# Block 2's depthwise convolution: three of its eight channel blocks as TensorE matmuls, and GpSimd's work moved out of the norm before it

## The chip, the core and the metric

The kernel runs on one core of one Trainium2 chip. The metric is the device time of one execution in microseconds (us). The engines are named as the profile names them: PE (TensorE), DVE (VectorE), ACT (ScalarE), POOL (GpSimd) and SP, whose queue issues the weight loads.

## What is computed

Two transformer blocks run over 256 tokens of 1024 features. The change lies at the end of block 1 and in the first half of block 2. There, as the reference has it:

```python
def conformer_conv(a, b, w_dw, b_dw, ln_g, ln_b, w_pw2, b_pw2):
    u = a * jax.nn.sigmoid(b)
    u = lax.conv_general_dilated(
        u, w_dw[:, None, :], window_strides=(1,), padding=[(CONV_TAPS - 1, 0)],
        dimension_numbers=('NWC', 'WIO', 'NWC'), feature_group_count=CONV_WIDTH) + b_dw
    u = jax.nn.silu(layer_norm(u, ln_g, ln_b))
    return u @ w_pw2 + b_pw2
```

The convolution is depthwise and causal, with 31 taps: each of the 1024 channels has its own 31 weights, and its output at a token is a sum over that token and the 30 before it. `a` and `b` are two slices of one projection of the normed activations; the same projection yields queries, keys, values and two gates. Differential attention runs beside the convolution, the two gated results are added, projected by `w_out` and added to the residual. A routed mixture of 64 experts closes the block.

## The kernel before, in words

**Stages.** Block 1 with its experts ends at about 415 us. Then come the gate that closes block 1 (`put_pg`, L1651), the norm that opens block 2, the projections, the convolution and the attention (about 416 to 702 us), the two output projections (to 756 us), and block 2's experts (to the end). All weights come over SP's queue in tiles of 1 MB through a ring; a tile's place is loaded again when the tile has been used.

**Pieces.** A projection is cut into pieces of half a weight tile. A piece first splits its weights in two (`parts`, L506): ACT rounds a 128x1024 half to fp32r (`whi`, L513) and another engine subtracts to get the low part (`wlo`, L514). Then 24 matmuls (L548 or L558) make hi times hi, hi times lo and lo times hi. The low part is DVE's by default; `split["eng"]` gives it to POOL in some places. `fill` runs the next piece and prepares the splits of the two behind it; `ready(n, eng)` prepares the first n queued pieces at once. There are three buffers of each part.

**Order.** Every engine runs its instructions in program order, and the order is written by hand. `step` (L1700) runs one piece and then some convolution taps; there is one `step` inside the norm, 15 in a first loop and 48 in a second (64 in all, numbered 0 to 63 below). The table `WHEN` at the top says how many taps follow each step (`v`, `v0` for DVE, `p`, `p0` for POOL) and at which step each part of the attention and of the layer norm is emitted. The pieces are, in order: 16 for the convolution's inputs (`cb`, `ca`), 40 for queries, keys, values and gates, 8 of the modulation vectors (`ada`). After the 64 steps come the two output projections.

**The convolution.** `put_ca` (L1715) writes `u`, two blocks of 128 channels at a time, and queues 31 taps for each block. Blocks 1, 2, 4, 5 and 7 are DVE's: the last tap is a `tensor_scalar` with the bias (L1691), the other 30 are a `scalar_tensor_tensor` each (L1693), 128x256 elements. Blocks 0, 3 and 6 (`ON_POOL`) take their first product from DVE; then, for each of 30 taps, ACT multiplies by the weight (`tap`, L1696) and POOL adds (L1697). `conv_end` flushes what is left, and POOL adds the blocks for the layer norm (`added`, L1925).

**The norm before it.** In the last `put_pg` (j = 3) DVE makes `h` (L1659), and just before that `ready(5, P)` lets POOL make the low part of the first `cb` piece. After the sums of squares, `ready(4, P)` lets POOL make the low part of the first `ca` piece; DVE and ACT write the scaled transposable copy `xp` (L414, L416) beside it. POOL then scales `h` in place (L1772).

**Queries and keys.** `put_qk` and `rotate` form a chain: ACT squares, DVE sums, POOL adds and takes a power (`rr`, L1788), DVE scales (`qn`, L1794), POOL rotates (L1799 to L1801), PE transposes (L1809).

Of the kernel before, what the change touches and what calls it, by code (L numbers as in the profile page):

```python
# [7 lines left out]
F32 = mybir.dt.float32  # L8
# [4 lines left out]
OP = mybir.AluOpType  # L13
# [3 lines left out]
T = 256  # L17
# [6 lines left out]
            v=(4, 4, 3, 3, 3, 4, 3, 3, 3, 4, 4, 4),  # L24
            p=(2, 2, 1, 2, 2, 3, 2, 1, 2, 3, 2, 1),
            v0=(3, 3, 3, 3, 3),
            p0=(2, 2, 2, 2, 2),
            pool=(12, 32),
# [9 lines left out]
AHEAD = 2  # L38
ON_POOL = (0, 3, 6)
TWO_PI = 6.283185307179586  # L40
# [155 lines left out]
def two_blocks(ctx, tc, I, out):  # L196
# [1284 lines left out]
    def pre_a():  # L1481

        dwT = pr.tile([128, 8, 34], F32, name="dwT")
        ps = wk([128, 8, 34], "dw")
        for j in range(8):
            PE.transpose(ps[:, j], pre["crow"][:, 128 * j:128 * j + 128], ident[0:34, 0:34])
        V.tensor_copy(dwT, ps)
        pT = pr.tile([128, 2, T], F32, name="pT", tag="pT")
        ps = wk([128, 2, T], "tr")
        for k in range(2):  # L1490
            for tt in range(2):
                PE.transpose(ps[:, k, 128 * tt:128 * tt + 128], pre["pin"][:, tt, 128 * k:128 * k + 128], ident)
        V.tensor_copy(pT, ps)
        V.tensor_scalar(pre["sub"], pre["sub"], 1.0 - 0.2, None, op0=OP.mult)
        lsum = pr.tile([128, 2], F32, name="lsum")
        lj = pr.tile([128, 64], F32, name="lj")
        lam4 = pre["lam4"]
        for i in range(2):
            V.scalar_tensor_tensor(lj, lam4[:, 2 * i], 1.0, lam4[:, 2 * i + 1], op0=OP.mult, op1=OP.mult,
                                   accum_out=lsum[:, i:i + 1])  # L1500
# [150 lines left out]
    def put_pg(j, ps):  # L1651
        c = slice(256 * j, 256 * j + 256)
        sg = t2.tile([128, 2, 256], F32, name="sg")
        S.activation(sg, ps, AF.Sigmoid)
        if j == 3:
            ready(5, P)
        V.tensor_tensor(sg, pps[0][:, :, c], sg, op=OP.mult)
# [21 lines left out]

    taps = {V: [], P: []}  # L1680

    def conv_some(eng, n):
        q = taps[eng]
        for _ in range(n):
            if not q:
                return
            i, tap = q[0].pop(0)
            q[:2] = [x for x in q[1::-1] if x]
            src, w = u[:, i, tap:tap + T], dwT[:, i, tap:tap + 1]
            if tap == 30:  # L1690
                V.tensor_scalar(acc[:, i], src, w, dwT[:, i, 31:32], op0=OP.mult, op1=OP.add)  # L1691
            elif eng is V:
                V.scalar_tensor_tensor(acc[:, i], src, w, acc[:, i], op0=OP.mult, op1=OP.add)  # L1693
            else:
                t = t2.tile([128, T], F32, name="tap", bufs=4)
                S.activation(t, src, AF.Copy, scale=w)  # L1696
                P.tensor_tensor(acc[:, i], acc[:, i], t, op=OP.add)  # L1697

    def step(n, v, p, eng=V):
        for _ in range(n):  # L1700
            split["eng"] = eng
            fill()
            split["eng"] = V
            conv_some(V, v)
            conv_some(P, p)

# [8 lines left out]
    def put_ca(j, ps):  # L1715
        V.tensor_tensor(u[:, 2 * j:2 * j + 2, 30:], ps, sgl.pop(j), op=OP.mult)
        for i in (2 * j, 2 * j + 1):
            eng = P if i in ON_POOL else V
            taps[eng].append([(i, tap) for tap in [30] + list(range(30))])

# [11 lines left out]
    put_proj()  # L1732
    fill(9)
    ssum = sm.tile([128, 2, 2], F32, name="ssum")
# [5 lines left out]
    P.tensor_tensor(r4, rt, halfneg[:, 0:2], op=OP.pow)  # L1740
    ready(4, P)
    r = sm.tile([128, 2], F32, name="rstd")
# [14 lines left out]
    for k, ps in turned(xp):  # L1757
        if k == 4:
            step(1, 0, 0)
# [6 lines left out]
    u = a2.tile([128, 8, 30 + T], F32, name="u")  # L1766
    P.memset(u[:, :, 0:30], 0.0)
    x_acc, acc = acc, a2.tile([128, 8, T], F32, name="acc")
    bpw = pr.tile([128, D], F32, name="bpw", tag="finalg")
    P.dma_start(out=bpw, in_=bcast_rows(l0("b_pw2_2")))  # L1770
    for tt in range(2):
        P.tensor_scalar(h[:, tt], h[:, tt], r[:, tt:tt + 1], None, op0=OP.mult)  # L1772

# [39 lines left out]
    vv = a2.tile([128, 2, D], F32, name="vv")  # L1813
    sgc = a2.tile([128, 2, D], F32, name="sgc")
    sga = a2.tile([128, 2, D], F32, name="sga")
    def put_gc(j, ps):
        S.activation(sgc[:, :, 256 * j:256 * j + 256], ps, AF.Tanh, scale=0.5)

# [12 lines left out]
    for n in range(15):  # L1831
        step(1, WHEN['v0'][n // 3], WHEN['p0'][n // 3])

# [170 lines left out]
    def conv_end():  # L2004
        conv_some(V, 1000)
        conv_some(P, 1000)
        ln_s()
# [13 lines left out]
    for n in range(48):  # L2021
        step(1, 0, 0, P if n in WHEN["pool"] else V)
        for fn, args in sorted(after.get(n, ()), key=lambda x: WHEN["rank"].index(x[0].__name__)):
            fn(*args)
        conv_some(V, WHEN["v"][n // 3] if n < 36 else 0)
        conv_some(P, WHEN["p"][n // 3] if n < 36 else 0)
    ln["m"] = [a2.tile([128, 8, T], F32R, name="xm" + n, tag=t) for n, t in (("hi", "kT"), ("lo", "xp"))]
# [182 lines left out]
```

## Time and profile before

| | us |
|---|---|
| median of 3 runs (1255.69 to 1259.72) | 1256.07 |
| the profiled execution | 1257.67 |
| its span, first to last instruction | 1255.9 |
| busy in the span: PE / DVE / ACT / POOL | 1128.7 / 598.4 / 412.2 / 243.8 |
| chain that ended last: PE / DMA / DVE / POOL | 50% / 27% / 15% / 3% |

The chain follows the work that ended last back from the final instruction, at each step to what released it. An engine's busy time is an average over stages, so the stage that the change touches is read by itself. Matmuls are pipelined: one lasts longer than the time until the next starts.

### The profile page before, as it was taken

To read this page: it belongs to the slowest core of one execution; us is meant where nothing else is said; L and a number is where in the kernel's file an instruction comes from. 1 tells how busy PE (TensorE), PEld (TensorE's weight loads), DVE (VectorE), ACT (ScalarE), POOL (GpSimd) and SP (SyncE) were. 2 spreads that over 40 slices of the span, in tenths; PEclk is the share of its full clock that TensorE was granted. 3 is DMA by queue.
4 is the path that set the end of the run, shared out by engine and by line. 5 is a ranking of instruction groups with operands and counts; after the bars stand their busy time and mean duration, and the time that the engine had idled before them with its cause. 6 is when DMAs were issued, how large, how long until landed. Compare 5 with 4: busy or idle time off the path is not lost.

```text
span 1255.9 us, 22423 instructions
## 1 busy us (share of the span) xinstructions
PE 1128.7 (90%) x8571; PEld 751.2 (60%) x8571; DVE 598.4 (48%) x1303; ACT 412.2 (33%) x823; POOL 243.8 (19%) x300
## 2 busy tenths in 40 slices
PE   6999989996777779888887898999999999998997
PEld 5998765652324678887877795444444444344443
DVE  5764652331110679999997765222322222221223
ACT  4464441210101666665655443112111111111111
POOL 5020140000000156694965511000000000000000
PEclk9999999998788989999989898999999999998999
DMA  9874889999999764434433959799999999999995
GB/s 284 250 246 155 327 299 345 390 419 418 419 419 398 262 210 168 156 115 133 134 102 107 357 202 399 312 400 421 420 421 421 420 420 421 420 420 420 420 420 218
DMA packets 115789, 398.34 MB, mean 317 GB/s; under 512 B 7681, under 2 KB 67181, under 8 KB 79440
## 3 DMA queue, kind: packets, MB, share of 16 engines
q1 hardware_dynamic: 113216, 392.72, 80.5%
q0 software_dynamic: 2448, 4.03, 1.4%
q8 instruction: 70, 1.15, 0.4%
q14 instruction: 55, 0.45, 0.1%
HBM read 395.63 MB, written 1.06 MB: 316 GB/s over the span
## 4 chain that ended last, share of the span: by engine, by line
PE 50%; DMA 27%; DVE 15%; POOL 3%; issue 3%; ACT 2%; SPq 0%; ACTq 0%; POOLq 0%; DVEq 0%
DMA w<-in_w_exp_gu_dram 12%; PE gu L1255 10%; PE fk L548 9%; PE dn L1306 7%; DVE acc L1693 4%; DMA w<-in_w_up_dram 4%; DVE wlo L514 4%; PE fk L558 4%; PE ga L1222 4%; DMA w<-in_w_exp_down_dram 3%; DMA w<-in_w_gate_dram 3%; PE y L1315 3%; DMA w<-in_w_down_dram 3%; PE gu L1264 3%; PE ak L548 1%
## 5 line engine op out<-in xcount | busy, mean ns | idle before, releaser
L1255 PE MATMUL gu<-w,xg 128*32 128x512 f32 (+2 forms) x1440 | 208.0, 600 | 9.7 <-DMA w<-in_w_exp_gu_dram 9.6
L1277 DVE SCALAR_TENSOR_TENSOR hh<-sg,wslot,gu 128x256 f32<-128x256 f32 x38 | 25.8, 678 | 281.7 <-ACT sg L1275 281.7
L514 DVE TENSOR_TENSOR wlo<-w,whi 128x1024 fp32r<-128x1024 f32 (+2 forms) x111 | 140.8, 1278 | 36.2 <-ACT whi L513 36.1
L1255 PEld LDWEIGHTS gu<-w,xg 128*32 128x32 f32 (+2 forms) x1440 | 63.7, 118 | 149.5 <-issue 136.2
L1306 PE MATMUL dn<-w,hT 128*32 128x512 f32 (+2 forms) x976 | 151.0, 605 | 2.0 <-DMA w<-in_w_down_dram 1.6
L513 ACT ACTIVATE whi<-w 128x1024 fp32r<-128x1024 f32 (+2 forms) x116 | 118.8, 1032 | 41.9 <-PE fk L548 23.0
L1264 PE MATMUL gu<-w,xg 128*32 128x256 f32 (+1 forms) x1024 | 93.0, 436 | 32.2 <-DMA w<-in_w_gate_dram 13.3
L1275 ACT ACTIVATE sg<-gu 128x256 f32<-128x256 f32 x38 | 14.6, 384 | 314.1 <-PE gu L1255 202.6
L1309 DVE TENSOR_TENSOR ylo<-dn,yhi 128x512 fp32r<-128x512 f32 x76 | 52.6, 692 | 127.0 <-ACT yhi L1308 127.0
L548 PE MATMUL fk<-wlo,x4hi 128*128 128x256 f32 x320 | 93.3, 291 | 13.0 <-DVE wlo L514 12.2
L548 PE MATMUL fk<-whi,x4hi 128*128 128x256 f32 x320 | 94.6, 296 | 3.7 <-DVE qn L1794 3.3
L1697 POOL TENSOR_TENSOR acc<-acc,tap 128x256 f32<-128x256 f32 x90 | 85.7, 967 | 48.2 <-ACT tap L1696 43.0
L1264 PEld LDWEIGHTS gu<-w,xg 128*32 128x32 f32 (+1 forms) x1024 | 48.3, 132 | 76.7 <-issue 22.3
L548 PE MATMUL fk<-whi,x4lo 128*128 128x256 f32 x320 | 91.9, 287 | 0.0
L1693 DVE SCALAR_TENSOR_TENSOR acc<-u,dwT,acc 128x256 f32<-128x256 f32 x150 | 89.8, 641 | 0.8
L2168 POOL DMA_DIRECT2D w<-gd x1 | 0.6, 638 | 460.4 <-DMA w<-in_w_exp_gu_dram 460.4
L1306 PEld LDWEIGHTS dn<-w,hT 128*32 128x32 f32 (+2 forms) x976 | 40.5, 118 | 78.2 <-issue 70.8
L1308 ACT ACTIVATE yhi<-dn 128x512 fp32r<-128x512 f32 x76 | 45.4, 597 | 121.9 <-PE dn L1306 121.9
L548 PEld LDWEIGHTS fk<-wlo,x4hi 128*128 128x128 f32 x320 | 62.8, 196 | 15.0 <-DVE wlo L514 13.9
L1315 PE MATMUL y<-yhi,dT 128*128 128x512 f32 x152 | 64.7, 426 | 1.7 <-ACT yhi L1308 1.5
L548 PEld LDWEIGHTS fk<-whi,x4hi 128*128 128x128 f32 x320 | 62.9, 197 | 4.6 <-ACT vv L1827 2.0
L548 PEld LDWEIGHTS fk<-whi,x4lo 128*128 128x128 f32 x320 | 62.9, 197 | 0.0
(604 smaller groups left out, 2316.5 us busy)
## 6 DMA issues: line engine op xcount, KB each, us to landing
w<-in_w_exp_gu_dram SPq DMA_DIRECT2D x128, 1024.0 KB, 19.8
w<-in_w_exp_down_dram SPq DMA_DIRECT2D x60, 1024.0 KB, 19.8
w<-in_w_in_dram SPq DMA_DIRECT2D x37, 1024.0 KB, 5.4
w<-in_w_gate_dram SPq DMA_DIRECT2D x32, 1024.0 KB, 18.4
w<-in_w_up_dram SPq DMA_DIRECT2D x32, 1024.0 KB, 17.5
w<-in_w_down_dram SPq DMA_DIRECT2D x28, 1024.0 KB, 19.5
w<-in_w_ada_dram SPq DMA_DIRECT2D x24, 1024.0 KB, 5.1
w<-in_w_down_dram SPq DMA_DIRECT2D x8, 512.0 KB, 13.6
```

The costliest lines, as they stand in the source:

```text
L513: S.activation(hi, w, AF.Copy)
L514: split.get("eng", V).tensor_tensor(lo, w, hi.bitcast(F32), op=OP.subtract)
L548: PE.matmul(ps[:, tt, :n], lhsT=xs[a], rhs=w[b][:, k], skip_group_check=True, start=(i + tt + k + m == 0), stop=(i == 1 and k == 3 and m = ...
L558: PE.matmul(ps[:m, b], lhsT=w[a][:, k, m * b:m * b + m], rhs=x[c][:, 4 * i + k], skip_group_check=True, start=(i + b + k + z == 0), stop=( ...
L1222: PE.matmul(ps[:, j], lhsT=xx[:, tt, k], rhs=d[:, tt], start=(i == 0), stop=(i == 3))
L1255: PE.matmul(ps[off:off + w, :], lhsT=xg[:, k, o + off:o + off + w], rhs=gu_of(q0 + qi, k), start=(k == 0), stop=(k == 7))
L1264: PE.matmul(ps[off:off + w, 256 * part:256 * part + 256], lhsT=xg[:, k, o + off:o + off + w], rhs=of(q0 + qi, k), start=(k == 0), stop=(k ...
L1306: PE.matmul(ps[off:off + w, :], lhsT=hT[g][:, k, off:off + w], rhs=down_of(q0 + qi, k, f, last), start=(k == 0), stop=(k == 1))
L1309: V.tensor_tensor(lo[:, f], ps, hi[:, f].bitcast(F32), op=OP.subtract)
L1315: PE.matmul(y[tt][f], lhsT=DT[g][:, 128 * tt:128 * tt + 128], rhs=v[:, f], start=False, stop=(g == NG - 1 and i == 1), skip_group_check=True)
L1693: V.scalar_tensor_tensor(acc[:, i], src, w, acc[:, i], op0=OP.mult, op1=OP.add)
L1697: P.tensor_tensor(acc[:, i], acc[:, i], t, op=OP.add)
```

## The change

Blocks 0, 3 and 6 of the convolution become matmuls. For each of them POOL's queue copies `u` to DRAM and reads it back four times, shifted by 0 to 3 tokens, so that 128 partitions hold 4 shifts of 32 channels; POOL multiplies the tap weights into diagonal 32x32 matrices; 32 matmuls (8 groups of 4 taps, 4 groups of 32 channels) sum all taps into PSUM, and ACT adds the bias on the way out. They are emitted at steps 9, 15 and 22. The layout of the weights (`w4`) is made once during block 1's experts. ACT's and POOL's 90 taps and DVE's first products of these blocks go.

In the norm, the low part of the first `cb` piece is made by DVE and earlier (`ready(7, V)` after five fills), that of the first `ca` piece by DVE (`ready(4, V)`), and POOL's scaling of `h` is moved to after the eleventh step of the first loop. The gate tile `sgc` takes the memory of `u4` afterwards.

```diff
-            p=(2, 2, 1, 2, 2, 3, 2, 1, 2, 3, 2, 1),
-            p0=(2, 2, 2, 2, 2),
+            conv={9: 0, 15: 1, 22: 2},
...
+        for j in range(4):
+            for m in range(4):
+                PE.matmul(ps[32 * m:32 * m + 32, j], lhsT=ident[:, 32 * j:32 * j + 32],
+                          rhs=dwT[:, ON_PE[0]:ON_PE[-1] + 1:ON_PE[1] - ON_PE[0], m:m + 29:4], start=True, stop=True)
+        w4 = pr.tile([128, 4, n, 8], F32, name="w4")
+        V.tensor_copy(w4, ps)
...
-        if j == 3:
-            ready(5, P)
...
-                t = t2.tile([128, T], F32, name="tap", bufs=4)
-                S.activation(t, src, AF.Copy, scale=w)
-                P.tensor_tensor(acc[:, i], acc[:, i], t, op=OP.add)
...
+    def conv_load(n):
+        ud = gd.tile([128, UW], F32, name=f"ud{n}")
+        P.dma_start(out=ud, in_=u[:, ON_PE[n]])
+        u4 = a2.tile([128, 2, D], F32, name="u4", tag="sgc").rearrange("p a b -> p (a b)")[:, 0:4 * (T + 28)]
+        u4 = u4.rearrange("p (j t) -> p j t", j=4)
+        w = t2.tile([128, 8, 4, 32], F32, name="cw", bufs=1)
+        for m in range(4):
+            P.dma_start(out=u4[32 * m:32 * m + 32], in_=ud.rearrange("(j c) t -> c j t", j=4)[:, :, m:m + T + 28])
+        P.tensor_tensor(w, pre["w4"][:, :, n].rearrange("p j g -> p g j")[:, :, :, None].to_broadcast([128, 8, 4, 32]),
+                        pre["each"][:, None, None, :].to_broadcast([128, 8, 4, 32]), op=OP.mult)
+        cw[n] = u4, w
+
+    def conv_pe(n):
+        u4, w = cw.pop(n)
+        i = ON_PE[n]
+        ps = wk([128, T], "cv")
+        for g in range(8):
+            for j in range(4):
+                PE.matmul(ps[32 * j:32 * j + 32], lhsT=w[:, g, j], rhs=u4[:, j, 4 * g:4 * g + T], start=(g == 0), stop=(g == 7))
+        S.activation(acc[:, i], ps, AF.Identity, bias=dwT[:, i, 31:32])
+        if n + 1 in cw_due:
+            cw_due.remove(n + 1)
+            conv_load(n + 1)
...
-            conv_some(V, v)
-            conv_some(P, p)
+            if steps[0] in WHEN["conv"]:
+                conv_pe(WHEN["conv"][steps[0]])
+            steps[0] += 1
+            conv_some(v)
...
-    fill(9)
+    fill(5)
+    ready(7, V)
+    fill(4)
...
-    ready(4, P)
+    ready(4, V)
...
-    for tt in range(2):
-        P.tensor_scalar(h[:, tt], h[:, tt], r[:, tt:tt + 1], None, op0=OP.mult)
...
-        step(1, WHEN['v0'][n // 3], WHEN['p0'][n // 3])
+        step(1, WHEN['v0'][n // 3])
+        if n == 10:
+            for tt in range(2):
+                P.tensor_scalar(h[:, tt], h[:, tt], r[:, tt:tt + 1], None, op0=OP.mult)
```

`put_ca` calls `conv_load` for block 0 at step 3; block 3 is loaded when block 0's matmuls have been emitted (step 9), block 6 after block 3's (step 15).

## Rows read from the trace of the kernel before

**Rows 1.** Busy time by stretch: PE, weight loads, DVE, ACT, POOL; granted clock; DMA share

```profile
225.00:230.00 5.00, 5.00 (x39) 3.26 (x35) 0.79 (x2) 0.38 (x1) 0.00 (x0) 1.00 1.00 392
465.00:688.00 223.00, 193.33 (x1540) 182.35 (x1542) 209.51 (x346) 131.73 (x278) 149.48 (x178) 0.98 0.40 133
641.00:688.00 47.00, 40.43 (x313) 38.49 (x317) 39.47 (x71) 20.53 (x49) 26.38 (x26) 0.91 0.34 112
756.00:1256.00 500.00, 480.33 (x3200) 228.43 (x3200) 146.50 (x422) 91.06 (x179) 4.03 (x3) 0.98 0.97 398
```

**Rows 2.** Waits of PE, 465 to 520 us and 520 to 688 us

```profile
PE fk L558 <- DVE wlo L514: 2.5, 5, 1.2
PE fk L548 <- DVE wlo L514: 1.1, 1, 1.1
...
PE fk L548 <- DVE wlo L514: 11.0, 7, 4.0
PE qt L1809 <- POOL qn L1801: 5.7, 6, 1.8
PE fk L548 <- DVE qn L1794: 3.3, 3, 1.2
PE po L1898 <- ACT aT L1890: 2.0, 2, 1.2
PE pvar L1951 <- POOL lnsum L1930: 1.6, 1, 1.6
```

**Rows 3.** Groups of instructions by line and shape, 465 to 688 us

```profile
L1693 DVE SCALAR_TENSOR_TENSOR acc<-u,dwT,acc 128x256 f32<-128x256 f32 x150 | 89.8, 641 | 0.8
L1697 POOL TENSOR_TENSOR acc<-acc,tap 128x256 f32<-128x256 f32 x90 | 85.7, 967 | 48.2 <-ACT tap L1696 43.0 <-ACT whi L513 3.6
L514 DVE TENSOR_TENSOR wlo<-w,whi 128x1024 fp32r<-128x1024 f32 x51 | 69.1, 1357 | 4.6 <-ACT whi L513 4.6
L1696 ACT ACTIVATE tap<-u,dwT 128x256 f32<-128x256 f32 x90 | 41.7, 509 | 14.2 <-POOL acc L1697 9.0 <-DVE u L1716 5.2
L514 POOL TENSOR_TENSOR wlo<-w,whi 128x1024 fp32r<-128x1024 f32 x2 | 4.9, 2460 | 0.0
```

**Rows 4.** DVE in order of time: start, duration, engine, line, operation

```profile
504.20 1.26 DVE L1693 SCALAR_TENSOR_TENSOR acc<-u,dwT,acc 128x256 f32<-128x256 f32 x3
505.38 1.21 DVE L514 TENSOR_TENSOR wlo<-w,whi 128x1024 fp32r<-128x1024 f32 x1
...
512.20 2.73 DVE L1693 SCALAR_TENSOR_TENSOR acc<-u,dwT,acc 128x256 f32<-128x256 f32 x3
```

**Rows 5.** POOL in order of time, same columns, and the idle time before

```profile
509.23 6.30 POOL L1697 TENSOR_TENSOR acc<-acc,tap 128x256 f32<-128x256 f32 x6 [6.97 <-ACT tap L1696]
```

**Rows 6.** The chain that ended last, from 689 us: start, duration, what

```profile
689.84 1.91 PE ad L898 x32
```

**Rows 7.** DVE around the norms in order of time, as rows 4

```profile
449.57 0.69 DVE L1658 TENSOR_TENSOR sg<-sg,h 128x512 f32<-128x512 f32 x1
450.30 2.74 DVE L1659 TENSOR_TENSOR h<-sg,finalg 128x512 f32<-128x512 f32 x1
...
455.09 3.39 DVE L414 TENSOR_SCALAR xp<-h,r 128x512 f32<-128x512 f32 x2 [0.83 <-POOL r L1740]
...
755.77 1.28 DVE L414 TENSOR_SCALAR xp<-h,rstd 128x512 f32<-128x512 f32 x2 [1.13 <-POOL rstd L384]
```

**Rows 8.** POOL in the norm, in order of time, as rows 5

```profile
449.78 2.71 POOL L514 TENSOR_TENSOR wlo<-w,whi 128x1024 fp32r<-128x1024 f32 x1 [1.75 <-ACT whi L513]
...
460.13 0.57 POOL L1770 DMA_DIRECT2D bpw<-in_b_pw_dram  x1
460.73 5.70 POOL L1772 TENSOR_SCALAR h<-h,rstd 128x1024 f32<-128x1024 f32 x2
```

**Rows 9.** DMA issues of POOL's queue: size each, median us from issue to landing

```profile
finalg<-in_final_g_dram POOLq DMA_DIRECT2D x1, 512.0 KB, 9.1
bpw<-in_b_pw_dram POOLq DMA_DIRECT2D x1, 512.0 KB, 4.0
```

More of the change, by code (lines that the diff above doesn't have):

```diff
@@ L38 @@
 AHEAD = 2
-ON_POOL = (0, 3, 6)
+ON_PE = (0, 3, 6)
 TWO_PI = 6.283185307179586
@@ L1487, in pre_a @@
         V.tensor_copy(dwT, ps)
+        n = len(ON_PE)
+        ps = wk([128, 4, n, 8], "w4")
+        for j in range(4):
[4 more added lines that the diff above has]
+        V.tensor_copy(w4, ps)
+        V.memset(w4[96:128, :, :, 7:8], 0.0)
+        each = pr.tile([128, 32], F32, name="each")
+        V.tensor_tensor(each, twice[:, 0:32], twice[:, 32:64], op=OP.add)
+        pre.update(w4=w4, each=each)
         pT = pr.tile([128, 2, T], F32, name="pT", tag="pT")
@@ L1677, in two_blocks, with conv_some @@
     queue(*ada(3, fk))
-    taps = {V: [], P: []}
-    def conv_some(eng, n):
-        q = taps[eng]
+    taps = []
+    def conv_some(n):
         for _ in range(n):
-            if not q:
+            if not taps:
                 return
-            i, tap = q[0].pop(0)
-            q[:2] = [x for x in q[1::-1] if x]
+            i, tap = taps[0].pop(0)
+            taps[:2] = [x for x in taps[1::-1] if x]
             src, w = u[:, i, tap:tap + T], dwT[:, i, tap:tap + 1]
@@ L1691, in conv_some, with step @@
                 V.tensor_scalar(acc[:, i], src, w, dwT[:, i, 31:32], op0=OP.mult, op1=OP.add)
-            elif eng is V:
+            else:
                 V.scalar_tensor_tensor(acc[:, i], src, w, acc[:, i], op0=OP.mult, op1=OP.add)
-            else:
-                t = t2.tile([128, T], F32, name="tap", bufs=4)
-                S.activation(t, src, AF.Copy, scale=w)
-                P.tensor_tensor(acc[:, i], acc[:, i], t, op=OP.add)
-    def step(n, v, p, eng=V):
+    UW = T + 32
+    cw = {}
+    def conv_load(n):
[20 more added lines that the diff above has]
+            conv_load(n + 1)
+    cw_due, steps = [], [0]
+    def step(n, v, eng=V):
         for _ in range(n):
@@ L1715, in put_ca @@
     def put_ca(j, ps):
-        V.tensor_tensor(u[:, 2 * j:2 * j + 2, 30:], ps, sgl.pop(j), op=OP.mult)
+        V.tensor_tensor(u[:, 2 * j:2 * j + 2, 30:30 + T], ps, sgl.pop(j), op=OP.mult)
         for i in (2 * j, 2 * j + 1):
-            eng = P if i in ON_POOL else V
-            taps[eng].append([(i, tap) for tap in [30] + list(range(30))])
+            if i not in ON_PE:
+                taps.append([(i, tap) for tap in [30] + list(range(30))])
+            elif ON_PE.index(i) == 0 or ON_PE.index(i) - 1 not in cw:
+                conv_load(ON_PE.index(i))
+            else:
+                cw_due.append(ON_PE.index(i))
     queue(*crossed(*(dense_feat(x4, (nm, j), 128, 2, lambda ps, j=j, put=put: put(j, ps))
@@ L1758, in two_blocks @@
         if k == 4:
-            step(1, 0, 0)
+            step(1, 0)
         S.activation(xs[0][:, k], ps, AF.Identity, scale=a1c[:, k:k + 1], bias=mod[:, 0, k:k + 1])
@@ L1765, in two_blocks @@
         V.tensor_tensor(xs[1][:, k], acc[:, k], xs[0][:, k].bitcast(F32), op=OP.subtract)
-    u = a2.tile([128, 8, 30 + T], F32, name="u")
+    u = a2.tile([128, 8, UW], F32, name="u")
     P.memset(u[:, :, 0:30], 0.0)
+    P.memset(u[:, :, 30 + T:], 0.0)
     x_acc, acc = acc, a2.tile([128, 8, T], F32, name="acc")
@@ L1813, in two_blocks @@
     vv = a2.tile([128, 2, D], F32, name="vv")
-    sgc = a2.tile([128, 2, D], F32, name="sgc")
     sga = a2.tile([128, 2, D], F32, name="sga")
+    ln = {}
     def put_gc(j, ps):
+        if j == 0:
+            ln["sgc"] = a2.tile([128, 2, D], F32, name="sgc")
+        sgc = ln["sgc"]
         S.activation(sgc[:, :, 256 * j:256 * j + 256], ps, AF.Tanh, scale=0.5)
@@ L1922, in two_blocks @@
     V.memset(onesf, 1.0 / D)
-    ln = {}
     def added(x):
@@ L1983, in put_pw @@
     def put_pw(j, ps):
+        sgc = ln["sgc"]
         c = slice(256 * j, 256 * j + 256)
@@ L2004, in conv_end @@
     def conv_end():
-        conv_some(V, 1000)
-        conv_some(P, 1000)
+        conv_some(1000)
         ln_s()
@@ L2021, in two_blocks @@
     for n in range(48):
-        step(1, 0, 0, P if n in WHEN["pool"] else V)
+        step(1, 0, P if n in WHEN["pool"] else V)
         for fn, args in sorted(after.get(n, ()), key=lambda x: WHEN["rank"].index(x[0].__name__)):
             fn(*args)
-        conv_some(V, WHEN["v"][n // 3] if n < 36 else 0)
-        conv_some(P, WHEN["p"][n // 3] if n < 36 else 0)
+        conv_some(WHEN["v"][n // 3] if n < 36 else 0)
     ln["m"] = [a2.tile([128, 8, T], F32R, name="xm" + n, tag=t) for n, t in (("hi", "kT"), ("lo", "xp"))]
```

## The prediction

> **What bounds the kernel now.** I read the busy time by stretch first. From 465 to 688 us the steps run: DVE is busy 209.51 of 223 us, PE 193.33, POOL 149.48 and ACT 131.73, and the DMA engines are at 0.40 [rows 1]. DVE is the fullest engine, but PE is close behind, so DVE's relief can give back only what PE loses: the 223 - 193.33 = 29.7 us in which PE idles. The waits of PE say on whom: low parts that DVE has late (2.5 + 1.1 + 11.0 = 14.6 us), the rotation of queries and keys (5.7 on POOL, 3.3 on DVE), attention on ACT (2.0) and a layer-norm sum on POOL (1.6) [rows 2]. Two of the waits for DVE are of 4 us, and behind them the granted clock falls: 0.91 as a mean from 641 to 688 us. At the half level, 1.2 GHz, half of the time is lost, so 47 x (1 - 0.91) = 4.2 us of PE's busy time there is slowness and no work [rows 1].
>
> After 756 us the DMA engines are at 0.97 for 500 us [rows 1]. That stretch is a stream of weights whose start is set by the stage before it, so a gain before 688 us should move the end by as much.
>
> **Why DVE is full.** The groups of instructions give 150 taps at a mean of 641 ns and 51 low parts at 1357 ns [rows 3]. In order of time the same forms have two durations. At 504.20 us three taps take 1.26 us and the low part after them 1.21; at 512.20 us three taps take 2.73 us [rows 4]. POOL is idle for 6.97 us up to 509.23 and then adds six taps in 6.30 us [rows 5]. So a DVE tap costs about 0.40 us beside an idle POOL (1.18 from the first start to the low part's start, over 3) and up to 0.88 beside a POOL tap.
>
> **The change, part by part.**
>
> *POOL's and ACT's taps go.* POOL sheds 90 additions, 85.7 us, ACT 90 products, 41.7 us [rows 3]. Neither is the fullest engine, so by themselves they are worth nothing; what counts is DVE. Were every DVE tap and low part undisturbed, the taps would take 150 x (0.56 - 0.40) = 24 us less (0.56 is the mean of 0.641 without the 0.08 by which the next instruction overlaps, as 504.20 + 1.26 overlaps 505.38 in rows 4) and the low parts 51 x (1.357 - 1.21) = 7.5 us, 32 us in all. But POOL keeps the rotation, the sums and some low parts. Its taps are 85.7 of its 149.48 us, 57%; some of the rest are powers of 8 elements that hardly touch memory, so I take two thirds, 21 us. DVE's 3 first products go too, 3 x 0.4.
>
> *What comes to POOL in the same stretch:* three weight products of 1024 elements, for which the nearest row is a low part on POOL, 2.46 us [rows 3], and the scaling of `h`, 5.70 us, moved from 460.73 us [rows 8] into step 11. That is 13 us which disturb DVE as the taps did, about 13 x 21/85.7 = 3 us of it back. DVE: 209.5 - 21 - 1 + 3 = 190 us.
>
> *PE gets three times 32 matmuls* with 32 weight columns and 256 moving columns, four column groups in turn. The `ad` matmuls are of this form: 32 took 1.91 us [rows 6]. So 3 x 1.91 = 5.7 us, all on the path, because PE runs in order and is next to full. ACT's evacuations, three of about half a microsecond by a tap's 509 ns [rows 3], hide in what ACT has shed.
>
> *PE then becomes the bound:* 193.33 - 4.2 + 5.7 = 194.8 us of work against DVE's 190. What idle time remains is the open number. The rotation, attention and sum waits (5.7 + 3.3 + 2.0 + 1.6 = 12.6) are chains over several engines; POOL's part of them loses its queue of taps, but PE arrives sooner and they are exposed for longer, so I leave them at 11. Of the 14.6 us on DVE's low parts I keep 3, and 1 for POOL's later answer behind the third load. Together 15 us. The ends are 0 (below that nothing can go, since idle time is not negative) and 29.7 with the clock's 4.2 (nothing relieved). I take 15, nearer to the sum of the chains than to either end. The stretch: 194.8 + 15 = 209.8 instead of 223, **13.2 us less**.
>
> *The norm before it.* DVE's last `h` took 2.74 us where the same size took 0.69 just before [rows 7], while POOL made a low part from 449.78 us [rows 8]. That low part is now made by DVE before the last gate arrives, so 2.05 us go. `xp` took 3.39 us for two beside POOL's next low part, 1.28 undisturbed at 755.77 [rows 7]: 2.1 us go. Ahead of it DVE gets that low part, 1.21 [rows 4]. Together 2.05 + 2.1 - 1.2 = **3 us**. ACT's share of the split is where it was.
>
> *The loads of the convolution* are a chain on POOL's queue: one copy to DRAM, a wait for its landing, four reads, one product. The trace has no such copy. The nearest row is a POOL load of 512 KB, 0.57 us to issue [rows 8] and 4.0 us to land [rows 9]; the slowest landing of its kind is 9.1 us [rows 9]. With those, 0.6 + 4.0 + 4 x 0.6 + 4.0 = 11 us, or 0.6 + 9.1 + 2.4 + 9.1 = 21 us. From the load's emission to its matmuls lie six steps (3 to 9, 9 to 15) or seven (15 to 22), each at least 24 matmuls: PE's 194.8 us over 56 steps are 3.5 us each, so 21 us. I take 11, since the DMA engines are as free as then, and cost the wait at nothing; the cover is those six pieces, and at the other end it is just used up. Behind the waits on POOL's queue stand the scaling of `h`, which nobody needs until the output projection, and at step 17 the first sum and power for the rotation: that is the 1 us above. Three loads of some 0.15 MB written and 0.6 MB read add about 2 MB to a stretch at 0.40; nothing.
>
> *The layout of the weights* adds 16 tiny matmuls and a wait for a DVE copy during block 1's experts, some 2 us of PE (16 at 1.91/32 [rows 6], and a wait taken as one low part's 1.2). At 225 to 230 us the DMA engines are at 1.00 [rows 1], so the weights behind it arrive no sooner: nothing, or 2 us if that queue ran dry.
>
> **Sum.** 1257.67 - 13.2 - 3 = 1241.5 for the profiled execution; its time is 1.6 above the median, so 1239.9, **1240 us**.
>
> **Rivals.**
>
> *The relief is only partly DVE's.* If POOL's remaining rotation disturbs as much for each microsecond as the taps, or the chains fill the idle time, 24 us stay idle: 194.8 + 24 = 218.8, 4.2 less, with the norm 7.2: 1249 us. For it: 9 of the waits are already POOL's and DVE's latency in the rotation. Against it: the largest two waits come where DVE is late with taps behind it.
>
> *Nothing is relieved.* DVE's long taps come from something other than POOL's additions; then PE's 5.7 us come on top and the norm's 3 go: 1259 us, no difference to be measured. Against it: rows 4 and 5 change together. That the change does not do what it says would look the same; the diff leaves no additions on POOL.
>
> *The loads are late,* and the time is worse than before. Each microsecond that a load exceeds 21 us stops PE, three times over, with every engine behind it. The gain of 16 us is used up when each is 5.4 us late, at a round trip of 26 us; from there it is slower. With landings of 13 us, 0.6 + 13 + 2.4 + 13 = 29 us, 8 us late each: 1240 + 24 = 1264 us. Against it: the landings of 4.0 us in this very stage [rows 9]. The Trainium skill (SBUF — State Buffer, "A bandwidth-pool intuition that's wrong") speaks for it: while DVE runs certain fp32 operations GpSimd is locked out of a port that it shares with DVE and cannot write the descriptors of a DMA on its queue, so that the transfer seems blocked. By that rule the load's issue, not its landing, would stretch, and the time would be the 1264 of this rival. The trace shows no sign of it so far: POOL issued its load at 460.13 us in 0.57 us [rows 8].
>
> **Chances.** Forecast 0.62, the partial relief 0.14, nothing 0.12, late loads 0.12. A measurement of this kernel can tell about 0.3%, 3.8 us, from no change: faster is under 1252.3, slower over 1259.8. Faster 0.62 + 0.14 = 0.76, same 0.12, slower 0.12. The range: below, PE's idle time falls to 6 us, 9 better than forecast: 1231. Above, it goes past the partial relief up to where nothing is relieved, short of it: 1257; left out are the late loads and the tails, under 0.2.
>
> **What would show each step.** DVE's taps in the stretch at a mean under 550 ns and its busy time near 190 us; PE's waits for low parts at about 3 us; the granted clock at 1.00 in it; `h` at 0.69 and `xp` at 1.3 us in the norm; 32 convolution matmuls in 1.9 us; the first of them waiting for no load. What would make the prediction wrong: taps that stay at 600 ns, a wait of PE for a load or for the weight product, rotation waits that grow by more than the low parts' shrink, or a stretch after 688 us that takes the gain back in waits for weights.

## The result, and the profile after

The kernel with the change takes 1238.05 us (median of 4, 1236.69 to 1239.81), the kernel before 1256.03 us beside it (median of 4): 18.0 us less. The ratio of the runs is 0.9846, 95% interval 0.9827 to 0.9865, which is 19.4 us; below, kernels are compared by such ratios. The profiled execution of after took 1236.69 us, the lowest of its four; that of before, 1257.67, lies 1.6 above its median. So the two profiles differ by 21.0 us, 3 more than the medians, and what is read from them below adds up to the larger number.

Busy time by stretch of the kernel after (columns as in [rows 1]): all steps, the first and second part of them, and the experts.

```profile
461.83:668.00 206.17, 198.47 (x1723) 186.67 (x1725) 179.54 (x343) 96.62 (x189) 83.39 (x106) 0.98 0.48 156
461.83:520.00 58.17, 58.17 (x553) 54.68 (x552) 47.46 (x71) 25.39 (x31) 20.48 (x21) 1.00 0.67 208
520.00:668.00 148.00, 140.31 (x1173) 132.00 (x1175) 132.08 (x273) 71.23 (x158) 62.90 (x86) 0.98 0.40 135
735.50:1235.00 499.50, 477.99 (x3200) 229.78 (x3200) 146.66 (x422) 92.10 (x180) 4.73 (x4) 0.98 0.97 399
```

PE's steps begin 3.3 us earlier than before, at 461.83. They took 222.2 us before (465.16 to 687.4, inside the stretch of [rows 1]) and take 206.17 now: 16 us less. That lead is kept: the experts' first `xp` starts at 736.23 us (in the chain below) instead of 755.77 [rows 7], 19.5 us earlier. The stream of the experts' weights keeps the DMA engines at 0.97 as before, and its end comes 20.9 us earlier (the span went from 1255.9 to 1235.0 us): a start that comes earlier moves the end by about as much. In the first 58 us PE has no idle time at all.

Waits of PE in the steps, of the kernel after (us in total, times, longest):

```profile
PE fk L547 <- DVE wlo L513: 3.6, 3, 2.4
PE pvar L2000 <- POOL lnsum L1979: 2.0, 1, 2.0
PE qt L1852 <- POOL qn L1844: 1.8, 2, 1.3
PE fk L547 <- ACT vv L1874: 0.4, 1, 0.4
```

These four are all (`wlo` is a low part, `lnsum` the layer norm's sum, `qn` a normed query or key, `vv` the values). Low parts that DVE has late cost 3.6 instead of 14.6 us, the rotation 1.8 instead of 9.0 [rows 2].

Groups of instructions of after in the steps (columns as in [rows 3]):

```profile
L1703 DVE SCALAR_TENSOR_TENSOR acc<-u,dwT,acc 128x256 f32<-128x256 f32 x150 | 75.0, 543 | 0.8
L513 DVE TENSOR_TENSOR wlo<-w,whi 128x1024 fp32r<-128x1024 f32 x51 | 62.5, 1228 | 13.7 <-ACT whi L512 13.7
...
L1727 PE MATMUL cv<-u,cw 128*32 128x256 f32 x192 | 11.0, 380 | 0.0
...
L1716 POOL DMA_DIRECT2D u<-ud x12 | 6.6, 558 | 15.9 <-PE cv L1727 6.8 <-PE fk L547 4.8 <-PE fk L557 4.3
...
L1717 POOL TENSOR_TENSOR cw<-w,each 128x1024 f32<-128x1024 f32 x3 | 6.1, 2031 | 0.0
```

The same 150 taps went from 641 to 543 ns, the same 51 low parts from 1357 to 1228. What DVE now waits for is ACT's rounding (13.7 us): it has caught up with its supplier. PE's matmuls of the convolution wait for nothing (0.0 in the last column).

DVE in the norm, in order of time, and POOL with the first load of the convolution (columns as in [rows 4] and [rows 5]):

```profile
450.63 0.69 DVE L1669 TENSOR_TENSOR h<-sg,finalg 128x512 f32<-128x512 f32 x1
...
452.98 1.23 DVE L513 TENSOR_TENSOR wlo<-w,whi 128x1024 fp32r<-128x1024 f32 x1 [0.24 <-ACT whi L512]
454.12 1.29 DVE L413 TENSOR_SCALAR xp<-h,r 128x512 f32<-128x512 f32 x2
```

```profile
471.75 0.55 POOL L1711 DMA_DIRECT2D ud<-u  x1 [13.95 <-issue]
476.63 2.22 POOL L1716 DMA_DIRECT2D u<-ud  x4 [4.33 <-PE fk L557]
478.88 2.02 POOL L1717 TENSOR_TENSOR cw<-w,each 128x1024 f32<-128x1024 f32 x1
```

`h` is down from 2.74 to 0.69 us and the two `xp` from 3.39 to 1.29 [rows 7]. In the first load, the reads start 4.9 us after the copy to DRAM was issued. The wait ahead of them is put down to a matmul that had long been done; it is the copy's landing (as the wait of 4.82 us in the cut kernel below shows, which is put down to it by name).

The chain that ended last, of after: the three blocks of the convolution, POOL's scalings at the end of the layer norm, and the start of the experts' stage.

```profile
487.74 3.59 PE cv L1727 x64
...
508.80 3.59 PE cv L1727 x64
...
534.74 3.59 PE cv L1727 x64
...
672.72 7.22 POOL acc L2021 x6
...
736.23 0.69 DVE xp L413
```

Each block of the convolution is 3.59 us of PE, in 64 records; the code issues 32 matmuls for it. So one such fp32 matmul leaves two records.

### The profile page after: what moved, and what is told of

It is laid out like the page before. It is cut to its first block, busy times and chain, and to the rows that moved or that the text cites. A ratio compares the mean times of both kernels' runs of the same rounds, so it can differ in the third digit from the quotient of the medians.

```text
span 1235.0 us, 22677 instructions
## 1 busy us (share of the span) xinstructions
PE 1131.1 (92%) x8795; PEld 757.5 (61%) x8795; DVE 565.9 (46%) x1305; ACT 377.7 (31%) x736; POOL 170.1 (14%) x227
## 4 chain that ended last, share of the span: by engine, by line
PE 33%; DMA 25%; DVE 9%; POOL 3%; ACT 2%; issue 2%; SPq 0%; ACTq 0%; POOLq 0%; DVEq 0%
DMA w<-in_w_exp_gu_dram 17%; PE gu L1254 8%; PE fk L547 6%; PE dn L1305 4%; PE fk L557 4%; DMA w<-in_w_up_dram 3%; PE y L1314 3%; DVE acc L1703 2%; PE ga L1221 2%; DVE wlo L513 2%; DMA w<-in_w_down_dram 2%; DMA w<-in_w_exp_down_dram 2%; DMA w<-in_w_gate_dram 2%; PE y L2119 1%; PE ak L547 1%
## 5 line engine op out<-in xcount | busy, mean ns | idle before, releaser
L513 DVE TENSOR_TENSOR wlo<-w,whi 128x1024 fp32r<-128x1024 f32 (+2 forms) x113 | 136.7, 1219 | 45.9 <-ACT whi L512 45.8
L1305 PE MATMUL dn<-w,hT 128*32 128x512 f32 (+2 forms) x976 | 148.0, 604 | 3.1 <-DMA w<-in_w_down_dram 2.8
L1274 ACT ACTIVATE sg<-gu 128x256 f32<-128x256 f32 x38 | 14.6, 385 | 313.1 <-PE gu L1254 202.8
L1703 DVE SCALAR_TENSOR_TENSOR acc<-u,dwT,acc 128x256 f32<-128x256 f32 x150 | 75.0, 543 | 0.8
L1221 PE MATMUL ga<-disp,xhi 128*128 128x256 f32 x304 | 63.3, 290 | 0.0
## 6 DMA issues: line engine op xcount, KB each, us to landing
w<-in_w_up_dram SPq DMA_DIRECT2D x32, 1024.0 KB, 17.3
```

The lines of the kernel that those rows point to most:

```text
L513: split.get("eng", V).tensor_tensor(lo, w, hi.bitcast(F32), op=OP.subtract)
L1221: PE.matmul(ps[:, j], lhsT=xx[:, tt, k], rhs=d[:, tt], start=(i == 0), stop=(i == 3))
L1305: PE.matmul(ps[off:off + w, :], lhsT=hT[g][:, k, off:off + w], rhs=down_of(q0 + qi, k, f, last), start=(k == 0), stop=(k == 1))
```

## The experiments

The theory: DVE was the fullest engine because POOL's additions hold it up; without them PE's waits go, and PE is next to full. Against it stood ACT's relief (90 products that the change takes away too), POOL's queue (the additions stood ahead of the rotation there), the norm, and late loads. Ratios are to the kernel before, run beside each on the same chip.

### The norm alone, and the convolution alone

The kernel before with the norm's edits (`norm_only`), and the kernel after with them undone (`conv_only`):

```diff
-        if j == 3:
-            ready(5, P)
...
-    fill(9)
+    fill(5)
+    ready(7, V)
+    fill(4)
...
-    ready(4, P)
+    ready(4, V)
...
-    for tt in range(2):
-        P.tensor_scalar(h[:, tt], h[:, tt], r[:, tt:tt + 1], None, op0=OP.mult)
...
+        if n == 10:
+            for tt in range(2):
+                P.tensor_scalar(h[:, tt], h[:, tt], r[:, tt:tt + 1], None, op0=OP.mult)
```

These are the edits of `norm_only`; `conv_only` is the kernel after with the same lines turned back.

> The kernel before with the norm's part of the change alone: the two low parts on DVE, and the scaling of h after step 11; the convolution as before. My theory: the norm gives 3 us (h at 0.69 instead of 2.74, two xp in 1.3 instead of 3.4, one low part of 1.2 inserted), and the moved scaling, 5.7 us of POOL, now disturbs DVE and delays POOL's taps in the steps, up to 3 us back: 1253 to 1256 us. Rival, that most of the 18 us comes from the norm: 1245 or less. Rival, that the norm's gain is lost again in the steps, where DVE is full: 1256.

> The changed kernel with the norm as before: the low parts on POOL, the scaling of h in the norm; the convolution as changed. My theory: the convolution gives the rest, about 15 of the 18 us: 1240 to 1243 us, with h at 2.7 and the two xp at 3.4 us again. Rival, that the two parts need each other (the steps are short of DVE and POOL either way): the two parts alone add up to clearly less than 18 us, and this one is at 1246 or more.

Measured: the norm alone 1255.91 us, 0.9985 (0.9972 to 0.9997); the convolution alone 1241.33 us, 0.9869 (0.9852 to 0.9886). That is 1.9 and 16.5 us, 18.4 together, against 19.4 for both (0.0154 of 1257). The parts add, within what the intervals leave open; both runs lie in the range of the theory, the norm alone at its upper end, where its second rival lies too. In `norm_only` `h` takes 0.69 and `xp` 1.3 us as they do in after, but the two scalings of `h`, which now stand among POOL's and DVE's taps, take 3494 ns each instead of 2.85 us [rows 8], and the taps 646 ns: some of what the norm gives up is paid back in the steps. Beside the change's emptier POOL they take 2.93 us each.

### Which of the removed parts relieves DVE

The kernel after, with 90 operations put back where the taps were: additions on POOL over tiles of their own (`pool_adds_back`), products on ACT into a scratch tile (`act_products_back`), and fills on POOL, which write as much and read nothing (`pool_memsets`). Nobody waits for any of them.

```diff
+    def more(n):
+        for _ in range(n):
+            if extra[0] and steps[0] > 4:
+                extra[0] -= 1
+                P.tensor_tensor(dum[0], dum[0], dum[1], op=OP.add)
...
             conv_some(v)
+            more(p)
```

`act_products_back` has this as its last line of `more`, and `pool_memsets` `P.memset(dum[0], 0.0)`:

```diff
+                S.activation(t2.tile([128, T], F32, name="tap", bufs=1), u[:, 1, 0:T], AF.Copy, scale=dwT[:, 1, 0:1])
```

> The changed kernel, with 90 additions of 128x256 given back to POOL, in the places of the old ones, on two tiles of POOL's own that nobody else touches. My theory: DVE's taps and low parts are slow because POOL's additions read and write memory at the same time, so the mean tap goes from 543 back to about 640 ns and DVE's busy time in the steps from 180 to about 205 us; PE then waits for low parts by 10 to 15 us again: 1249 to 1260 us. Rival, that the gain came from ACT being freed of its products: the taps stay under 560 ns and the time at 1238 to 1241. Rival, that it came from POOL's queue, whose additions stood ahead of the rotation: the taps stay, and only PE's waits for the rotation grow, 1241 to 1246.

> The changed kernel, with 90 products of 128x256 given back to ACT, in the places of the old ones, into a tile that nobody reads. My theory: ACT was at 132 of 223 us before and is at 97 of 206 now, and its products do not touch DVE's speed: the mean tap stays within 10 ns of 543 and the time at 1237 to 1242 us. Rival, that ACT's high parts came late behind the products and held up DVE and PE: 1246 us or more, with waits of DVE for high parts.

> The changed kernel with 90 memsets of 128x256 given to POOL in the places of the old additions; they write memory and read none. My theory, that POOL's reading and writing beside DVE is what slows DVE, says nothing on writes alone; two forms of it: if it is the reading, DVE's mean tap stays under 560 ns and the time at 1238 to 1243 us; if writing does as much, the tap goes over 600 ns and the time over 1247. Rival, that the time is lost because POOL's queue makes the loads and the rotation wait, whatever it runs: PE's waits for the rotation and for the query and key banks grow and the time is over 1247 with taps under 560 ns.

Measured: additions 1269.9 us, 1.0112 (1.0092 to 1.0133), 10 us above the expected range; products 1240.02 us, 0.9862 (0.9847 to 0.9876); fills 1240.79 us, 0.9862 (0.9845 to 0.9879), both in the range of the theory. The groups in the steps, first with the additions, then the products, then the fills:

```profile
L1703 DVE SCALAR_TENSOR_TENSOR acc<-u,dwT,acc 128x256 f32<-128x256 f32 x150 | 94.4, 671 | 0.8
L1741 POOL TENSOR_TENSOR dum<-dum,dum 128x256 f32<-128x256 f32 x90 | 82.8, 920 | 5.2
```

```profile
L1703 DVE SCALAR_TENSOR_TENSOR acc<-u,dwT,acc 128x256 f32<-128x256 f32 x150 | 72.9, 529 | 0.8
...
L1741 ACT ACTIVATE tap<-u,dwT 128x256 f32<-128x256 f32 x90 | 45.5, 506 | 1.5
```

```profile
L1703 DVE SCALAR_TENSOR_TENSOR acc<-u,dwT,acc 128x256 f32<-128x256 f32 x150 | 71.8, 521 | 0.8
...
L1741 POOL MEMSET dum<- 128x256 f32 x90 | 28.2, 313 | 3.8
```

The additions alone bring back the long taps, 671 ns, though they share no tile and no wait with DVE. ACT's products, as long as they were before (506 ns), leave the taps at 529. Low parts have a mean of 1327 ns in that kernel, but two of the 51 make the difference: one of 3.18 and one of 4.25 us that lie beside POOL's weight product and a scaling of `h`. The ACT rival falls. Ninety fills leave the taps at 521: it is POOL's reading of SBUF that costs DVE time. The order of time shows how, DVE then POOL with the additions, and DVE then POOL with the fills:

```profile
472.71 1.52 DVE L1703 SCALAR_TENSOR_TENSOR acc<-u,dwT,acc 128x256 f32<-128x256 f32 x3
...
477.88 4.93 DVE L1703 SCALAR_TENSOR_TENSOR acc<-u,dwT,acc 128x256 f32<-128x256 f32 x3
482.73 1.76 DVE L513 TENSOR_TENSOR wlo<-w,whi 128x1024 fp32r<-128x1024 f32 x1
```

```profile
477.91 1.99 POOL L1717 TENSOR_TENSOR cw<-w,each 128x1024 f32<-128x1024 f32 x1
479.84 1.64 POOL L1741 TENSOR_TENSOR dum<-dum,dum 128x256 f32<-128x256 f32 x2
...
481.79 8.53 POOL L1741 TENSOR_TENSOR dum<-dum,dum 128x256 f32<-128x256 f32 x8
```

```profile
483.81 1.22 DVE L513 TENSOR_TENSOR wlo<-w,whi 128x1024 fp32r<-128x1024 f32 x1
```

```profile
483.37 2.89 POOL L1741 MEMSET dum<- 128x256 f32 x8
```

Three taps take 1.52 us while POOL does nothing, and 4.93 us beside the weight product and the additions behind it. The product's 1.99 us, two additions of about 0.8 and three taps of 0.4 to 0.5 make 4.8 to 5.1 us: as if the two engines took turns, one whole instruction each. A low part takes 1.76 us beside additions and 1.22 beside fills. The Trainium skill (SBUF — State Buffer, "Who interferes with whom") says that a VectorE instruction with two inputs in SBUF contends with a GpSimd instruction that reads SBUF and not with one that only writes it. These rows agree. The Trainium skill (SBUF — State Buffer, "SBUF: two separate sides") also says that whichever starts first holds the shared port pair for its whole instruction. The product and the additions agree; POOL's scalings of `h` in after, which read SBUF too, do not:

```profile
495.92 5.85 POOL L1882 TENSOR_SCALAR h<-h,rstd 128x1024 f32<-128x1024 f32 x2
```

```profile
497.78 1.21 DVE L513 TENSOR_TENSOR wlo<-w,whi 128x1024 fp32r<-128x1024 f32 x1
```

A low part that lies almost whole inside the first scaling takes no longer than beside an idle POOL, and the scalings take 5.85 us instead of 5.67 (in `short_cover`, beside an idle DVE). So not every reading instruction of POOL holds DVE up; why these do not stays open.

The additions made the kernel slower than before, which had the same number of them. The longest waits of PE in that kernel:

```profile
PE fk L547 <- DVE wlo L513: 9.0, 3, 4.5
PE fk L547 <- DVE qn L1849: 6.7, 1, 6.7
```

Low parts are late again, and one `qn` costs 6.7 us: POOL has the loads and the weight products on top of the additions now, and q's power stands behind them. So the additions cost in two ways, through DVE's speed and through POOL's queue, and both come back with them. How the 19.4 us divide between the two is not shown: the fills keep POOL busy for 28.2 us where the additions keep it for 82.8, too little to load its queue as before. PE's waits fell by 11.0 us for low parts and by 7.2 for the rotation.

### Is PE the bound now?

Only the first of eight groups of taps is multiplied, 4 of 32 matmuls; loads and weight products stay (`conv_cut`).

```diff
-        for g in range(8):
+        for g in range(1):
...
-                PE.matmul(ps[32 * j:32 * j + 32], lhsT=w[:, g, j], rhs=u4[:, j, 4 * g:4 * g + T], start=(g == 0), stop=(g == 7))
+                PE.matmul(ps[32 * j:32 * j + 32], lhsT=w[:, g, j], rhs=u4[:, j, 4 * g:4 * g + T], start=True, stop=True)
```

> The changed kernel with 4 of each block's 32 convolution matmuls (the first group of taps; the other seven groups are left out of the sum), loads and weight products as they are. A block's 32 matmuls took 3.59 us on PE. My theory: PE is the bound in the steps now, above all in the first 58 us where it has no wait at all, so 3 x 3.59 x 28/32 = 9.4 us of PE work come off nearly whole: 7 to 10 us under the changed kernel, 1228 to 1232 us. Rival, that DVE (180 of 206 us) is as much of a bound: under 5 us, 1234 or more.

Measured: 1234.0 us, 0.9816 (0.9801 to 0.9831). Of PE's three times 3.59 us, seven eighths went, 9.4 us; the time fell by 3.8 (0.0030 of 1257). Waits of PE in this kernel, steps and projections behind them, and POOL around the third load:

```profile
PE fk L547 <- DVE wlo L513: 4.1, 4, 2.4
PE fk L547 <- ACT whi L512: 3.9, 1, 3.9
PE fk L547 <- DVE qn L1837: 3.6, 1, 3.6
```

```profile
508.01 0.61 POOL L1711 DMA_DIRECT2D ud<-u  x1 [8.35 <-DVE u L1754]
513.44 2.20 POOL L1716 DMA_DIRECT2D u<-ud  x4 [4.82 <-DMA ud<-u]
515.66 1.99 POOL L1717 TENSOR_TENSOR cw<-w,each 128x1024 f32<-128x1024 f32 x1
...
519.27 1.67 POOL L1831 TENSOR_TENSOR rr<-ss,half 128x8 f32<-128x8 f32 x1
```

So 5.6 us came back. New is the wait for `qn`, 3.6 us: its power `rr` stands on POOL behind the third load. Low parts cost 4.1 instead of 3.6, and ACT's rounding 3.9 in the first piece behind the steps, where after waits 3.2 for another:

```profile
PE fk L547 <- DVE mrow L906: 3.2, 1, 3.2
```

These make 4.8 of the 5.6 us. In after, then, PE and the chains over POOL, DVE and ACT are level to within a few us, and PE's work is only partly the bound. The time lies on the rival's side.

### Two blocks on PE instead of three

```diff
-            v=(4, 4, 3, 3, 3, 4, 3, 3, 3, 4, 4, 4),
-            v0=(3, 3, 3, 3, 3),
-            conv={9: 0, 15: 1, 22: 2},
+            v=(4, 4, 4, 4, 4, 4, 3, 3, 4, 4, 4, 4),
+            v0=(4, 4, 4, 4, 4),
+            conv={9: 0, 22: 1},
-ON_PE = (0, 3, 6)
+ON_PE = (0, 6)
```

> The changed kernel with two blocks on PE (0 and 6) and block 3 back on DVE, 31 taps more, mostly in the first loop (4 taps a step). My theory: PE is the bound and loses 3.6 us, DVE gets 31 x 0.43 = 13 us, of which some 10 fit into the 10.7 us that it idles in the first 58 us of the steps; so 1 to 3 us under the changed kernel, 1235 to 1237. Rival, that DVE's bursts already set PE's waits: PE's waits for low parts grow by more than 3.6 us, 1240 to 1248.

Measured: 1246.49 us, 0.9916 (0.9902 to 0.9929), 8.8 us more than with three blocks. PE saves 3.6 us and DVE gets 30 taps more (180 at 530 ns). PE's waits for low parts up to 690 us are 7.1 us where three blocks have 3.9, and single waits of 4.1 us each for `lnsum` and `qn` have grown or come. This is the rival's range: DVE is not so far below PE that it could take a block back.

### The cover of the loads

The three blocks' matmuls earlier (`short_cover`), and the third block's load and matmuls later, out of the way of q's power (`late_third_load`):

```diff
-            conv={9: 0, 15: 1, 22: 2},
+            conv={5: 0, 9: 1, 17: 2},
```

```diff
-            conv={9: 0, 15: 1, 22: 2},
+            conv={9: 0, 15: 1, 28: 2},
...
-        if n + 1 in cw_due:
+        if n + 1 in cw_due and n == 0:
...
+            if steps[0] == 21:
+                conv_load(cw_due.pop())
```

> The changed kernel with the convolution's matmuls two steps after their load is emitted (steps 5, 9, 17 instead of 9, 15, 22). From the changed kernel's trace a load takes 0.6 to issue, about 4.5 to land, 2.2 for four issues, then 2.0 for the product beside 4.3 for the landing: 11.5 us. Two pieces cover 5.8 to 6. My theory: PE waits about 5 us at each of the three, DVE and the rest catch up in it, so the time rises by 10 to 15 us: 1248 to 1254. Rival (the price of late loads is small, since the engines behind PE use the wait): under 5 us, 1243 or less. Rival (the round trip is longer, about 21 us, and was only just covered): over 30 us, 1268 or more.

> The changed kernel with block 6's load emitted at step 21 instead of 15, and its matmuls at step 28 instead of 22: behind the first rotation of queries and keys on POOL's queue and no longer ahead of it. In the run with the matmuls cut PE waited 3.57 us for the first queries, whose power stood behind that load; in the changed kernel the chain that ended last runs through the load, the product and that power. My theory: POOL's queue there costs 1 to 3 us: 1235 to 1237. Rival, that PE and DVE are level and the load's place is free: 1238. Rival, that the load now stands ahead of the second rotation or the attention: 1239 to 1242.

Measured: 1267.38 us, 1.0074 (1.0058 to 1.0089), slower than before and than the theory had it, and 1239.26 us, 0.9861 (0.9846 to 0.9876), no gain over after. In `late_third_load` PE has a wait for `qn` of 2.4 us that after does not have: a power of the rotation stands behind the load now, as the last of its rivals has it. Of `short_cover`: the waits of PE, its group of convolution matmuls, and the first load on POOL.

```profile
PE cv L1727 <- DMA u<-ud: 25.6, 3, 9.3
```

```profile
L1727 PE MATMUL cv<-u,cw 128*32 128x256 f32 x192 | 16.9, 527 | 25.6 <-DMA u<-ud 25.6
```

```profile
470.20 0.55 POOL L1711 DMA_DIRECT2D ud<-u  x1 [14.35 <-issue]
475.24 2.22 POOL L1716 DMA_DIRECT2D u<-ud  x4 [4.49 <-PE fk L557]
```

```profile
483.18 6.31 PE L1727 MATMUL cv<-u,cw 128*32 128x256 f32 x64 [8.51 <-DMA u<-ud]
```

Each load comes about 8.5 us late, 25.6 in all, and the matmuls behind the wait are slower: 6.31, 5.34 and 5.20 us instead of 3.59 for a block, up to 637 ns for a record that takes 379 in after, at a granted clock of 0.57 in those 6.31 us, most of the way to TensorE's half level (1.2 of 2.4 GHz); in after the same 64 records have 1.00. The total of the group grows by 5.9 us. Together that is 31.5 us, of which 28.7 show (0.0228 of 1257). The round trip of the first load is read here without cover: from its issue at 470.20 to the matmul at 483.18 are 13.0 us. In after the first load is issued at 471.75 and needed at 487.74, so it lands with some 3 us to spare.

So the round trip is 13 us and not 21, and the rival with 21 falls. Expected were 5 us of lateness for each load. It was 8.5, because a load takes 13.0 us and not 11.5, and because the copy is issued 1.2 us after the piece ahead of it ends.

Where a copy is issued is set by `u`, which DVE writes only when a piece's matmuls are done. In `short_cover` the three loads are emitted right behind that write (steps 3, 7 and 15), two steps ahead of their matmuls. The third copy:

```profile
533.58 0.61 POOL L1711 DMA_DIRECT2D ud<-u  x1 [21.23 <-DVE u L1754]
```

Its matmuls start at 546.87, 13.3 us later. In after, block 3's copy is issued at 484.26, as soon as its `u` is written and ahead of block 0's matmuls; only its reads wait for these (the 6.8 us in the groups above), since they fill the same tile. It has 24.5 us until its matmuls and block 6's has 24.2 (510.53 to 534.74), so the first load is the tightest.

### Less of the layer norm's scaling on POOL

After the steps POOL scales six blocks in 7.22 us on the chain. Four were left to it (`fewer_pool_scales`), DVE took two more; then with the late third load as well (`both_moves`).

```diff
-            lnp=(1, 3, 4, 5, 6, 7),
+            lnp=(1, 3, 5, 7),
```

> The changed kernel with four of the eight scalings before the last nonlinearity of the layer norm on POOL instead of six (blocks 1, 3, 5, 7), the other four on DVE. In the changed kernel's chain POOL's six take 7.22 us, from 672.72 to 679.94, and the first pw matmul waits for what follows; in the kernel before a weight load of 8.77 us stood in their place. My theory: the steps end earlier than the loads after them can follow, so the ends of POOL's chain and of the w_pw load lie close together, and 2 to 3 us off POOL's chain bring 0.5 to 2 us: 1236 to 1238. Rival, that the load ends the wait alone: no difference, 1238. Rival, that DVE's own queue there (12.3 of 14 us) is the bound: 1239 to 1240.

> The two moves together: block 6's load at step 21 with its matmuls at step 28, and four scalings on POOL. If both bring what my theory says, they touch different stretches and add: 1234 to 1236 us. If only the end of the steps matters (rival: a gain in the steps is taken back in the wait for weights after them), it is no better than the better of the two alone.

Measured: with four scalings on POOL 1235.12 us, 0.9831 (0.9818 to 0.9845), the lowest of all kernels that compute the whole sum; with both 1238.81 us, 0.9856 (0.9837 to 0.9876). The first is 1.9 us under after, and the intervals overlap, so it is likely but not shown to be better. In its trace the first piece behind the steps starts 0.95 us earlier than in after (681.27 instead of 682.22), as the theory has it; the time lies just under its range. The late third load adds nothing to it: with both, the wait for `qn` is there again (2.3 us).

## Why the prediction was right

1240 us was forecast, 1238.05 measured, inside the range, and the mechanism that carried the forecast is the one that the runs show: POOL's additions slowed DVE, and without them most of PE's waits go. That the number came so close is in part luck, since terms that were mis-sized cancel. Between the two profiles 16.2 us were forecast and 21.0 measured. The terms beside what the traces of before and after show:

| term | forecast | measured |
|---|---|---|
| the steps | 209.8 | 206.2 |
| PE's work without the convolution | 189.1 | 187.7 |
| the convolution on PE | 5.7 | 10.8 |
| PE's idle time | 15 | 7.7 |
| DVE's busy time | 190 | 179.5 |
| the norm | -3 | -3.3 |
| behind the steps | 0 | -1.6 |

**The cause** holds. "Nothing is relieved" fell with the additions put back, which alone brought the long taps and the late low parts again. The forecast put all of the relief down to DVE; POOL's emptier queue, which shortens the rotation by itself, it set off against a PE that arrives sooner. Its share is not shown.

**DVE.** The two thirds of the undisturbed 32 us that the prediction took, 21 us, are what taps and low parts lost: 89.8 - 75.0 + 69.1 - 62.5 = 21.4 us. What it left out are DVE's other operations: the softmax's six groups fell from 25.6 to 17.3 us in the same stretch, the 128x128 scaling of `ex` (a `tensor_scalar`) from 643 to 360 ns for one. The forecast looked only at the two largest groups.

**The convolution on PE** was mis-sized, and by the reading of a row: `ad` x32 in [rows 6] are 32 records, taken for 32 matmuls, and are 16. "3 x 1.91 = 5.7 us" should have been twice that; measured 3 x 3.59 = 10.8.

**PE's idle time** was mis-sized the other way. For low parts 3 us were kept and 3.6 measured. The chains were left at 11, on the ground that a PE that arrives sooner exposes them; they came to 4.2 (2.0 + 1.8 + 0.4). The waits show that they got shorter by more than PE gained on them; that this is POOL's emptier queue and the faster softmax is argued, not shown. The two errors, 5.1 us too little work and 7.3 too much idle time, cancel but for 2.2; the last 1.4 are in PE's other busy time.

**The clock** was to come back to 1.00 and give 4.2 us. It did not: it is 0.98 over the steps as before, and 0.93 over their last 48 us.

```profile
620.00:668.00 48.00, 43.36 (x337) 41.34 (x339) 38.65 (x79) 21.64 (x52) 18.05 (x17) 0.93 0.36 130
```

So 48 x (1 - 0.93) = 3.4 us of slowness are left and 0.8 went. The waits that are left are shorter (2.42 us up to 645.85 and 1.98 up to 662.93, where before two of 4 us stood), but behind the first the granted clock is 0.67 from 645.85 to 651.00, and behind the second 0.67 from 662.93 to 668.10. The term was made up for by another that the forecast left out: for the same 1531 records, PE was busy 192.57 us before (465.16 to 687.40) and is 187.7 now, 4.9 us less. A matmul's record is 0.28 us long and the next starts after 0.12, so every wait fewer takes 0.16 from the busy time, and 28 waits became 7: 3.4 us. With the clock's 0.8 that is 4.2; the last 0.7 stay open.

**"PE then becomes the bound"** was half true. Taking 9.4 us of its work away gave 3.8.

**The norm.** 2.05 + 2.1 - 1.2 was forecast, and `h`, `xp` and the low part that came in measure 0.69, 1.29 and 1.23 as taken. By runs the norm's edits give 1.9 us in the kernel before and 2.9 beside the convolution's (0.9869 - 0.9846 = 0.0023 of 1257).

**The layout of the weights** costs at most 0.3 us: DVE's last `h` starts at 450.63, before at 450.30 [rows 7].

**The loads.** "11 us" was the chain of issues and landings, measured 13.0 from issue to matmul. "Six pieces, 21 us" of cover was too much: 16.0 us for the first load. The 3.5 us for each step spread all of PE's work in the stretch over its 56 pieces, the attention of the later steps too; a piece by itself is 24 matmuls at 0.12 us, 2.9 us. Six are 17.2, and the copy is issued 1.2 us into them. So the cost of nothing held by 3 us, not by 10. The rival's price was sound: 8 us late each was to give 1264, and 8.5 us late each gave 1267. Its other support did not show. By the rule of the Trainium skill (SBUF — State Buffer, "A bandwidth-pool intuition that's wrong") GpSimd's issues would have stretched while DVE ran an instruction like the `tensor_copy` that it measures. The copies took 0.55 to 0.61 us to issue with DVE busy for 47.46 of the 58.17 us in which all three lie. Most of that time are taps and low parts with two inputs, not copies, so the trace shows no sign of the rule and does not test it either.

**Behind the steps**, 1.6 us more were gained, where nothing was forecast. Of these, 1.4 lie behind the experts' first `xp`. This is within what two profiled executions differ by, and stays open.

**The range** was said to leave out under 0.2. With its upper end at 1257 it leaves out "nothing is relieved" (1259) as well as the late loads: 0.24 by the forecast's own chances.

## What to carry to other kernels

An engine that is nobody's bottleneck can still be what slows one: before costing the removal of GpSimd work at nothing, compare the same VectorE instruction in the order of time beside an idle GpSimd and beside one that reads SBUF, for the GpSimd instructions in question. Count instructions in the code against records in the trace before multiplying a row, for fp32 matmuls above all. For a transfer that is to hide behind other work, take the cover from the schedule as it will be after the gain, and from the moment when its input is written.

## What was not expected of the hardware

GpSimd's fills of 128x256 cost VectorE nothing (521 ns for a tap beside 90 of them, 543 without), its additions of the same size 128 ns on every tap (671). Small operations suffered too: the 128x128 scaling of `ex` takes 643 ns before, 360 in after, 632 with the additions put back and 372 with the fills. And a wait of PE costs more than its length: after a wait of 8.51 us the same 64 records took 6.31 instead of 3.59 us, and after one of 1.98 us in after 24 matmuls took 4.50 instead of 2.9 us. GpSimd's scalings of 128x1024, though they read SBUF, left a low part inside them at 1.21 us.
